# Scores, values and states of the sample rows on four column quarters, mixing biases from column sums, and scan rows scaled ahead of the norm

## The chip, the cores and the metric

One core of one Trainium2 chip runs the whole kernel as one program. The metric is the device time of one execution in microseconds; the kernel before was run three times. The engines are named as in the profile: PE is TensorE (matmuls; its weight loads are PEld), DVE is VectorE, ACT is ScalarE, POOL is GpSimd and SP is SyncE, which issues the DMAs here.

## The reference

One step of a hybrid decoder layer, for a prompt of 1024 positions and for 8 sample sequences of 4 positions each (32 rows), all in fp32, width 1024:

- `h = rmsnorm(x)`, and one input projection `h @ w_in` whose columns are split into the inputs of three branches.
- Branch A: `v = layernorm(gelu(v))`, then in chunks of 128 positions `mixed = w_s v + b_s` with a lower triangular `w_s` for each of 8 channel groups; out is `gelu(u) * mixed * silu(gate)`. As v is `xhat * g + b`, the part of `mixed` that comes from the layer norm's `b` is `b` times the row sums of `w_s`: together with `b_s` it is a bias that depends on channel and position only (the kernel's BM).
- Branch B: a causal convolution of width 4 with SiLU, then a chunked scan with 16 heads of 64 channels, 2 groups and a state of 128: inside a chunk `(C B^T * decay) (x dt)`, across chunks `C h`, and `h = decay h + B^T (x dt)`; then `y = (y + d_skip x) * silu(z)`, divided by its root mean square over each group's 512 channels and scaled by `ssm_norm_g`.
- Branch C: attention of 4 heads of 256 channels over 256 memory tokens, gated. The prompt uses keys and values projected from `mem_prompt`; each of the 8 sample sequences uses its own cached keys and values.
- `y = rmsnorm(x + concat(A, B, C) @ w_out)`. New states, convolution tails, memory keys and values, and the samples' v rows are returned too.

## The kernel before

The large projections are fp32 products made of three products each, of a high and a low part of both operands (`gemm3`, lines 339 to 341: high by high, high by low, low by high). The parts are made by `split` (L124 on ACT, L127 on DVE or POOL). After each step of the contraction `gemm3` calls `hook`: the counter grows by `pace["rate"]`, and for each whole number reached one step of the side work runs, that is, one generator goes on to its next `yield`. What a step issues lands in the engines' queues between main products. So the order on each engine is that of the text as this interleaving unrolls it, and every engine works its queue in order; a `yield` moves what follows it back by 1/rate hooks.

The main stages in order of time: load and norm of the rows with their transposes into pairs of high and low parts (`rn[t].s1a`, `s1b`, `s2`, to about 20 us), the projections of z and v, then the units that make a block product with 7 sub-products (`unit`), for the convolved columns from 225 to 360 us and for the queries and the two gates from 360 to 665 us. In that last stretch the side work is `side_chain` (L1768): `conv_samples`, `mem_prep`, `sample_scan`, `sample_scores`, `sample_values`, `gm_prep`, one after the other at rates of 1.25, and 0.32 in the stages with loads. Then come the units with the mixing products, the scan of the prompt between products of the gate (786 to 1003 us), the first output projection, the projection of the memory's keys and values with the loading and splitting of the scan's rows (L2104 to 2130), the second output projection with attention, and the last one with the final norm.

What the change touches:

- `samp_in` (L490) multiplies the 32 sample rows in four column tiles of 32 each, 256 columns at a time. It is not changed.
- `sample_scores` (L1569): 16 steps, each with a 512 KB load, 8 transposes of keys (L1602), two copies out of PSUM, and the products of two heads for the step before (L1587), 4 products in the two column tiles of these heads. An fp32 product stands in the trace as two records. `sample_values` (L1626) has 16 steps of 4 products (L1649) in the same way.
- `sample_scan` (L1360): for each of 8 sequences two products of 512 columns in column tiles 0 and 1 (L1469) collect `C h` in `accs`; then for each group `gate_norm` and after that the scaling.
- `gm_prep` (L1703): transposes of `w_s`, three operations of 32x1024 on DVE for the samples' v rows (L1738 to 1741), then BM from 16 products (L1746, L1747), of 128 rows of a broadcast `b` by `w_s` and of one row of ones by `b_s`.
- The scan (L1248) works on chunk i, while `sA(i + 1)` prepares the next. `gate_norm` (L1113) has a product on DVE, Square with a sum on ACT (L1120), and `rstd`. Rows of chunk i - 1 are transposed into a PSUM bank of the units (`y_T`), scaled on ACT out of it (`y_T2`, L1138, four parts) into the tile `sz`, and stored from there to `yb_d` (L1141). `sz` has one buffer and also takes the gate's load; `xsD` has three, and L1200 writes the one that is free next.

```python
r = y_T(p.xsD, 128, gp_, cp_ * 128, acc_bank())
...
s_.r = gate_norm(SC_.p, s_.xsD, sz, 128)
...
fs.append(y_T2(r, 128, gp_, cp_ * 128, sz))
```

- `loadB` and `splitB` (from L2076): loads of the scan's rows into three buffers; four tiles per group were kept in SBUF and stand in the same list.
- The tail: `rows_part` and `rows_fin` sum squares of the last block in parts that end at the column blocks named in `SQE`.

## Time and profile before

| | us |
|---|---|
| runs | 1336.42, 1339.17, 1339.26 (median 1339.17) |
| profiled execution | 1339.14 |
| its span in the profile | 1337.4 |
| PE busy | 1276.8 |
| DVE busy | 759.7 |
| ACT busy | 587.5 |
| POOL busy | 348.7 |

The span runs from the first to the last instruction of the profiled execution. Busy time is the sum over an engine's instructions, without overlaps; an engine that is busy for 95% of the span leaves 60 us in which it does nothing. A time line lists an engine's instructions with start, duration, engine, line, output and inputs by tile names, tile shape, and in brackets the idle time of the engine ahead of it with the instruction that ended it; with several instructions of one kind in a row, their count stands behind an x. The granted clock is given as a share of full speed, 2.4 GHz.

### The profile page before, as it was taken

How to read it: one execution, taken by the hardware profiler on the slowest of the kernel's cores; microseconds unless marked ns; L12 is line 12 of the kernel's file. 1: busy time of each engine (PE TensorE's matmuls, PEld its weight loads, DVE VectorE, ACT ScalarE, POOL GpSimd, SP SyncE). 2: the span in 40 equal slices, each digit the busy share in tenths (PEclk: the TensorE clock that was granted, in tenths of full speed). 3: DMA queues.
4: the chain of work that ended last, by engine and by line, in shares of the span. 5: the costliest groups of instructions: out<-in, count | busy, mean ns of one | idle time of the engine just before them, and what ended most of it. 6: DMA issues, size and time to landing. Idle time of an engine off the chain costs nothing.

```text
span 1337.4 us, 22025 instructions
## 1 busy us (share of the span) xinstructions
PE 1276.8 (95%) x8211; PEld 1075.5 (80%) x8211; DVE 759.7 (57%) x1258; ACT 587.5 (44%) x1227; POOL 348.7 (26%) x384
## 2 busy tenths in 40 slices
...
GB/s 242 75 84 98 139 93 46 88 106 102 125 176 159 190 109 268 119 233 155 109 194 165 201 200 164 76 126 127 175 89 150 267 230 220 170 191 245 179 139 98
DMA packets 210622, 204.68 MB, mean 153 GB/s; under 512 B 28124, under 2 KB 176688, under 8 KB 209492
## 3 DMA queue, kind: packets, MB, share of 16 engines
...
q8 instruction: 65, 1.06, 0.3%
...
q0 software_dynamic: 512, 0.13, 0.1%
...
## 4 chain that ended last, share of the span: by engine, by line
PE 73%; DVE 9%; DMA 8%; ACT 4%; issue 3%; POOL 2%; SPq 1%; POOLq 0%; ACTq 0%; DVEq 0%
PE ps_mm L339 19%; PE ps_mm L341 18%; PE ps_mm L340 18%; DVE ul L457 1%; PE ps_acc L1649 1%; PE ps_acc L1587 1%; DMA yb<-yb_d 1%; PE ps_sd L1849 1%; PE ps_sd L1602 1%; DMA sz<-z_d 1%; DMA y_d<-gt 1%; DMA cr<-c_d 1%; PE ps_sd L317 1%; PE ps_sd L1293 1%; PE ps_acc L490 1%
## 5 line engine op out<-in xcount | busy, mean ns | idle before, releaser
L449 ACT ACTIVATE uh<-wst 128x512 fp32r<-128x512 f32 x80 | 50.1, 628 | 96.1 <-PE ps_mm L340 77.6
L457 DVE TENSOR_TENSOR ul<-wr,uh 128x512 fp32r<-128x512 f32 x84 | 68.4, 814 | 39.8 <-ACT uh L449 39.8
L2370 POOL TENSOR_TENSOR xres<-xres,gfin 128x1536 f32<-128x1536 f32 (+3 forms) x6 | 14.4, 2396 | 274.9 <-DVE ys L2418 233.8
L127 DVE TENSOR_TENSOR wl<-wr,wh 128x512 fp32r<-128x512 f32 (+3 forms) x53 | 51.2, 987 | 60.7 <-ACT wh L124 60.1
L449 ACT ACTIVATE uh<-wr 128x512 fp32r<-128x512 f32 x84 | 52.4, 625 | 59.7 <-PE ps_mm L340 55.3
L457 DVE TENSOR_TENSOR ul<-wst,uh 128x512 fp32r<-128x512 f32 x80 | 61.4, 767 | 23.3 <-ACT uh L449 23.0
L339 PE MATMUL ps_mm<-bH,wh 128*128 128x384 f32 (+1 forms) x192 | 63.6, 331 | 3.8 <-ACT bH L124 3.8
L340 PE MATMUL ps_mm<-bL,wh 128*128 128x384 f32 (+1 forms) x192 | 62.2, 324 | 0.3 <-DVE bL L127 0.3
L341 PE MATMUL ps_mm<-bH,wl 128*128 128x384 f32 (+1 forms) x192 | 62.1, 323 | 0.0
L435 POOL TENSOR_TENSOR wst<-wr 128x512 f32<-128x512 f32 x20 | 26.9, 1343 | 124.9 <-DMA wr<-in_w_in_dram 38.7
L124 ACT ACTIVATE wh<-wr 128x512 fp32r<-128x512 f32 (+3 forms) x60 | 47.3, 815 | 25.0 <-PE ps_mm L340 13.6
L339 PE MATMUL ps_mm<-xT1H,uh 128*128 128x512 f32 x128 | 54.6, 426 | 2.0 <-ACT uh L449 2.0
L339 PE MATMUL ps_mm<-xB22H,uh 128*128 128x512 f32 x128 | 53.9, 421 | 1.5 <-ACT sz_s L1120 1.0
L1016 DVE SCALAR_TENSOR_TENSOR ps_sd<-raw,vecs,ps_sd 128x512 f32<-128x512 f32 x72 | 54.2, 752 | 1.7
L339 PE MATMUL ps_mm<-xB21H,uh 128*128 128x512 f32 x128 | 53.6, 419 | 1.2 <-ACT uh L449 1.2
L339 PE MATMUL ps_mm<-xB11H,uh 128*128 128x512 f32 x128 | 52.3, 409 | 0.0
L340 PE MATMUL ps_mm<-xT1L,uh 128*128 128x512 f32 x128 | 52.0, 406 | 0.0
L341 PE MATMUL ps_mm<-xT1H,ul 128*128 128x512 f32 x128 | 51.9, 405 | 0.1
L340 PE MATMUL ps_mm<-xB21L,uh 128*128 128x512 f32 x128 | 51.0, 398 | 0.0
L341 PE MATMUL ps_mm<-xB21H,ul 128*128 128x512 f32 x128 | 50.9, 397 | 0.0
L340 PE MATMUL ps_mm<-xB22L,uh 128*128 128x512 f32 x128 | 50.8, 397 | 0.0
L341 PE MATMUL ps_mm<-xB22H,ul 128*128 128x512 f32 x128 | 50.6, 395 | 0.0
...
## 6 DMA issues: line engine op xcount, KB each, us to landing
...
```

Of the source, the lines that this page charges most:

```text
L124: ACT.activation(out=H, in_=raw, func=AF.Copy)
L127: leng.tensor_tensor(out=L, in0=raw, in1=rb(H), op=ALU.subtract)
L317: PE.transpose(out=ps[:, i, :T], in_=self.xn[:T, k * 128:(k + 1) * 128], identity=ident[:T, :T])
L339: PE.matmul(out=ps, lhsT=lH, rhs=rH, start=(first and k == k0), stop=False)
L340: PE.matmul(out=ps, lhsT=lH, rhs=rL, start=False, stop=False)
L341: PE.matmul(out=ps, lhsT=lL, rhs=rH, start=False, stop=(last and k == k0 + kn - 1))
L435: POOL.tensor_tensor(out=t1, in0=A_(u, 2, 1), in1=A_(u, 2, 2), op=ALU.add)
L449: ACT.activation(out=h, in_=src, func=AF.Copy)
L457: eng.tensor_tensor(out=l, in0=src, in1=rb(h), op=ALU.subtract)
L490: PE.matmul(out=ps[32 * j:32 * j + 32, 0:256], lhsT=xs[:, 4 * r + j, :], rhs=R[r][:, j, :], start=(r == 0), stop=(r == 1), tile_position=( ...
L1016: DVE.scalar_tensor_tensor(out=ps, in0=raw[:, 512 * h + j:512 * h + j + 512], scalar=cw(ct, j), in1=ps, op0=ALU.mult, op1=ALU.add)
L2370: eng.tensor_tensor(out=t[:, 0:nf, c0:c0 + w], in0=t[:, 0:nf, c0:c0 + w], in1=gc.unsqueeze(1).to_broadcast([128, nf, w]), op=ALU.mult)
```

## The change

Eleven transposes of the identity are issued in three places of the start. Steps are added: four ahead of the samples' SiLU, one net in the loop that makes the samples' xdt, three ahead of their `gate_norm` (one behind it goes), three in `gm_prep`. The rate of the side work goes from 1.25 to 1.32, and in the values' stage from 0.32 to 0.16, where a step now does twice the work. Scores and values take all four heads of a sequence at once, in four column tiles; the state products take four tiles of 256 columns. BM comes from column sums of the transposed `w_s` (a product with a column of ones), copied into row 0 of r2, over `b_s` in row 1, and one product of two rows by g2, whose row 0 is `b` and row 1 is ones. In the scan `y_T2` is issued before the norm of the next chunk, and writes into the `xsD` it came from; the order of the three products of `C h` is turned; `lt_make` goes from DVE to ACT. Half of the low parts in `a_split` go from POOL to DVE. Kept rows are split directly, so that the three buffers serve loads alone from the first step on. The tail's parts end at column blocks 3, 6, 7.

```diff
@@ -643,6 +643,12 @@
+    def turn(n):
+
+        ps = acc_bank()
+        for _ in range(n):
+            PE.transpose(out=ps[:, 0:128], in_=ident, identity=ident)
+
@@ -700,8 +706,11 @@
     x_s1a(1)
+    turn(7)
     rn[0].s2(0)
+    turn(2)
     rn[0].s2(1)
+    turn(2)
     w_split(2)
@@ -1043,6 +1052,8 @@
             yield
+        for _ in range(4):
+            yield
         ACT.activation(out=cvs, in_=cvs, func=AF.Silu)
@@ -1065,7 +1076,7 @@
                 PE.transpose(out=ps[:27, i * 128:(i + 1) * 128], in_=csT[:, 4 * j + i, :], identity=ident)
-            csn = pool.tile([128, 512], F32, tag="csn", name="csn", bufs=2)[:27]
+            csn = pool.tile([128, 512], F32, tag="csn", name="csn", bufs=3)[:27]
             ACT.activation(out=csn, in_=ps[:27, :], func=AF.Copy)
@@ -1169,7 +1180,7 @@
             t = Lts[i] = SC_.p.tile([128, 128], F32R, tag="Lt", name="Lt", bufs=2)
-            DVE.tensor_scalar(out=t, in0=SB_.Lraw, scalar1=SB_.qmask[:, i % 4:i % 4 + 1], scalar2=None, op0=ALU.mult)
+            ACT.activation(out=t, in_=SB_.Lraw, func=AF.Copy, scale=SB_.qmask[:, i % 4:i % 4 + 1])
             l_rows(i + 4)
@@ -1274,7 +1285,9 @@
                 po = sd()
-                mm3(po, s_.CH, s_.CL, *hHL)
+                PE.matmul(out=po, lhsT=s_.CH, rhs=hHL[0], start=True, stop=False)
+                PE.matmul(out=po, lhsT=s_.CL, rhs=hHL[0], start=False, stop=False)
+                PE.matmul(out=po, lhsT=s_.CH, rhs=hHL[1], start=False, stop=True)
             else:
@@ -1309,20 +1322,19 @@
                 sE(i + 1, 1)
+            fs = []
             if i > 0:
...
                 r = y_T(p.xsD, 128, gp_, cp_ * 128, acc_bank())
+                fs.append(y_T2(r, 128, gp_, cp_ * 128, p.xsD))
             DVE.tensor_tensor(out=s_.xsD, in0=s_.xsD, in1=pd, op=ALU.add)
...
                 DVE.tensor_tensor(out=hHL[1], in0=hT, in1=rb(hHL[0]), op=ALU.subtract)
-            fs = []
             if c == 7:
                 fs.append(state_out(g))
-            if i > 0:
-                fs.append(y_T2(r, 128, gp_, cp_ * 128, sz))
             yield
@@ -1412,8 +1424,8 @@
             DVE.tensor_tensor(out=h3(xsD[:, cs]), in0=h3(ps[:32]), in1=hb(dsk_b[:32, 8 * j:8 * j + 8], 32, 8), op=ALU.mult)
-        for _ in range(2):
-            yield
+            yield
+        yield
         DVE.tensor_tensor(out=h3(xde), in0=h3(xdt), in1=hb(te_s, 32, NH), op=ALU.mult)
@@ -1465,9 +1477,10 @@
                     ACT.activation(out=hbt[:, k, :], in_=hbt[:, k, :], func=AF.Copy, scale=decT[:, k, b:b + 1])
-                for g in range(2):
-                    PE.matmul(out=accs[32 * g:32 * g + 32, :], lhsT=Cm[:, g, b * 32:(b + 1) * 32],
-                              rhs=hTb[g], start=(b == 0), stop=(b == 7), tile_position=(0, 32 * g))
+                for q in range(4):
+                    PE.matmul(out=accs[32 * q:32 * q + 32, 0:256], lhsT=Cm[:, q // 2, b * 32:(b + 1) * 32],
+                              rhs=hTb[q // 2][:, (q % 2) * 256:(q % 2 + 1) * 256], start=(b == 0), stop=(b == 7),
+                              tile_position=(0, 32 * q))
             ps = sd()
@@ -1496,7 +1509,7 @@
         f()
-        set_pace(1.25)
+        set_pace(1.32)
         sz_s = sp2.tile([128, 8, 128], F32, tag="hb", name="sz_s", bufs=4).rearrange("p k n -> p (k n)")[:32]
@@ -1507,12 +1520,15 @@
                           start=True, stop=True)
-            DVE.tensor_copy(out=t1[:, cs], in_=accs[32 * g:32 * g + 32, :])
+            for e in range(2):
+                q = 2 * g + e
+                DVE.tensor_copy(out=t1[:, q * 256:(q + 1) * 256], in_=accs[32 * q:32 * q + 32, 0:256])
             DVE.tensor_tensor(out=h3(t1[:, cs]), in0=h3(t1[:, cs]), in1=hb(ea_s[:, 8 * g:8 * g + 8], 32, 8), op=ALU.mult)
...
             DVE.tensor_tensor(out=xsD[:, cs], in0=xsD[:, cs], in1=t1[:, cs], op=ALU.add)
+            for _ in range(3):
+                yield
             rs.append(gate_norm(sp2, xsD[:, cs], sz_s[:, cs], 32))
-            yield
             yield
@@ -1580,20 +1596,19 @@
-        def scores(b, a):
-            kTb = kTs.pop((b, a))
+        def scores(b):
+            kT = [kTs.pop((b, a)) for a in range(2)]
             for dt in range(2):
-                for h in (2 * a, 2 * a + 1):
+                for h in range(4):
                     PE.matmul(out=psS[h * 32:(h + 1) * 32, :], lhsT=qm[:, 2 * h + dt, b * 32:(b + 1) * 32],
-                              rhs=kTb[:, 2 * (h - 2 * a) + dt, :], start=(b == 0 and dt == 0), stop=(b == 7 and dt == 1),
+                              rhs=kT[h // 2][:, 2 * (h % 2) + dt, :], start=(b == 0 and dt == 0), stop=(b == 7 and dt == 1),
                               tile_position=(0, h * 32))
-        prev = None
         for b in range(8):
...
                 kb = kvq.pop(0)
-                kTb = sap.tile([128, 4, 256], F32, tag="kTb", name="kTb", bufs=2)
+                kTb = sap.tile([128, 4, 256], F32, tag="kTb", name="kTb", bufs=3)
                 for j in range(2):
@@ -1606,12 +1621,11 @@
                 kTs[b, a] = kTb
-                if prev is not None:
-                    scores(*prev)
-                prev = (b, a)
+                if b and not a:
+                    scores(b - 1)
                 yield
-        scores(*prev)
-        set_pace(1.25)
+        scores(7)
+        set_pace(1.32)
         yield
@@ -1638,20 +1652,20 @@
             yield
-        set_pace(0.32)
+        set_pace(0.16)
         psO = acc_bank()[:, 0:256]
         for b in range(8):
-            for a in range(2):
-                kv_load()
-                vb = kvq.pop(0)
-                for m in range(2):
-                    for h in (2 * a, 2 * a + 1):
-                        PE.matmul(out=psO[h * 32:(h + 1) * 32, :], lhsT=pm[:, m, h, b * 32:(b + 1) * 32],
-                                  rhs=vb[:, m, (h - 2 * a) * 256:(h - 2 * a + 1) * 256], start=(b == 0 and m == 0),
-                                  stop=(b == 7 and m == 1), tile_position=(0, h * 32))
-                yield
+            vb = [kvq.pop(0) for _ in range(2)]
+            for m in range(2):
+                for h in range(4):
+                    PE.matmul(out=psO[h * 32:(h + 1) * 32, :], lhsT=pm[:, m, h, b * 32:(b + 1) * 32],
+                              rhs=vb[h // 2][:, m, (h % 2) * 256:(h % 2 + 1) * 256], start=(b == 0 and m == 0),
+                              stop=(b == 7 and m == 1), tile_position=(0, h * 32))
+            kv_load()
+            kv_load()
+            yield
         DVE.tensor_copy(out=Psm, in_=psO)
-        set_pace(1.25)
+        set_pace(1.32)
         yield
@@ -1710,22 +1724,26 @@
             wsp = pp.tile([128, 8, 128], F32, name="wsp")
-            bsr = pp.tile([1, D], F32, name="bsr")
-            one_r = pp.tile([1, 128], F32, name="one_r")
+            g2 = pp.tile([2, D], F32, name="g2")
+            r2 = pp.tile([2, D], F32, name="r2")
+            one_c = pp.tile([128, 1], F32, name="one_c")
             rep = pp.tile([4, 8, 4], F32, name="rep")
-            gnb_b = pp.tile([128, D], F32, name="gnb_b")
+            gnb_b = pp.tile([32, D], F32, name="gnb_b")
             gng_b = pp.tile([32, D], F32, name="gng_b")
...
             SP.dma_start(out=wsp, in_=gm_w_spatial[0].rearrange("h t s -> t h s"))
-            SP.dma_start(out=gnb_b, in_=gm_norm_b.to_broadcast([128, D]))
+            POOL.memset(g2, 1.0)
+            SP.dma_start(out=g2[0:1], in_=gm_norm_b)
+            SP.dma_start(out=gnb_b, in_=gm_norm_b.to_broadcast([32, D]))
             SP.dma_start(out=gng_b, in_=gm_norm_g.to_broadcast([32, D]))
-            SP.dma_start(out=bsr, in_=gm_b_spatial[0].rearrange("h t -> (h t)").unsqueeze(0))
+            SP.dma_start(out=r2[1:2], in_=gm_b_spatial[0].rearrange("h t -> (h t)").unsqueeze(0))
             SP.dma_start(out=G.vsn, in_=v_d[NP:NT, :])
-            POOL.memset(one_r, 1.0)
+            POOL.memset(one_c, 1.0)
             POOL.memset(rep, 1.0)
...
             yield from conv_out(pp)
+            yield
             yield
@@ -1738,13 +1756,19 @@
             DVE.tensor_tensor(out=vs, in0=G.vsn, in1=gng_b, op=ALU.mult)
-            DVE.tensor_tensor(out=vs, in0=vs, in1=gnb_b[:NS], op=ALU.add)
+            DVE.tensor_tensor(out=vs, in0=vs, in1=gnb_b, op=ALU.add)
+            for j in range(2):
+                ps = sd()
+                PE.matmul(out=ps[0:1, :], lhsT=one_c, rhs=WT[:, 4 * j:4 * j + 4, :].rearrange("p h t -> p (h t)"),
+                          start=True, stop=True)
+                DVE.tensor_copy(out=r2[0:1, j * 512:(j + 1) * 512], in_=ps[0:1, :])
+            yield
+            yield
             for j in range(2):
...
                 for i in range(4):
-                    h = 4 * j + i
-                    PE.matmul(out=ps[:, i, :], lhsT=gnb_b[:, h * 128:(h + 1) * 128], rhs=WT[:, h, :], start=True, stop=False)
-                    PE.matmul(out=ps[:, i, :], lhsT=one_r, rhs=bsr[:, h * 128:(h + 1) * 128], start=False, stop=True)
+                    hs = slice((4 * j + i) * 128, (4 * j + i + 1) * 128)
+                    PE.matmul(out=ps[:, i, :], lhsT=g2[:, hs], rhs=r2[:, hs], start=True, stop=True)
                 DVE.tensor_copy(out=BM[:, 4 * j:4 * j + 4, :], in_=ps)
@@ -1787,7 +1811,7 @@
         pace["acc"] = 0.0
-        set_pace(1.25)
+        set_pace(1.32)
@@ -1974,7 +1998,7 @@
                 ACT.activation(out=H, in_=src, func=AF.Copy)
-                U.late.append((L, src, H, POOL if e else DVE))
+                U.late.append((L, src, H, DVE))
         return f
@@ -2070,20 +2094,22 @@
     ybp = yb_ctx.enter_context(tc.tile_pool(name="ybp", bufs=1, side="right"))
-    ytodo = ([(1, c) for c in range(KEEP, 8)] + [(g, c) for c in range(4) for g in range(2)] +
-             [(0, c) for c in range(4, NTILE)] + [(1, 8)])
+    ytodo = ([(g, c) for c in range(KEEP) for g in range(2)] +
+             [(0, c) for c in range(KEEP, NTILE)] + [(1, 8)])
...
             ytodo.pop(0)
-            if g and KEEP <= c < 8:
-                ybs.append((g, c, SC_.y[c].rearrange("p (k t) -> p k t", k=4)))
-                return
             t = ybp.tile([128, 4, 128], F32, tag="yb", name="yb", bufs=3)
...
             ybs.append((g, c, t))
+
+    def splitK(n):
+        c = KEEP + n
+        ts_ = slice(c * 128, c * 128 + 128)
+        split(SC_.y[c].rearrange("p (k t) -> p k t", k=4), bH[:, 4:8, ts_], bL[:, 4:8, ts_], ACT, DVE)
@@ -2118,11 +2144,11 @@
             if n < 4:
-                loadB()
-                splitB(0)
-            elif n < 15:
+                splitK(n)
+            if n < 15:
                 splitB(2)
-                loadB()
+                if n not in (3, 7, 11):
+                    loadB()
             else:
@@ -2398,7 +2424,7 @@
     side2 = Side()
-    SQE = [3, 5, 7]
+    SQE = [3, 6, 7]
     wo_get()
```

## Rows read from the trace of the kernel before

**Rows 1.** From the page: busy time of the engines, with share of the span and instructions; and the shares of the chain that ended last, by engine.

```profile
PE 1276.8 (95%) x8211; PEld 1075.5 (80%) x8211; DVE 759.7 (57%) x1258; ACT 587.5 (44%) x1227; POOL 348.7 (26%) x384
...
PE 73%; DVE 9%; DMA 8%; ACT 4%; issue 3%; POOL 2%; SPq 1%; POOLq 0%; ACTq 0%; DVEq 0%
```

**Rows 2.** The waits of PE: line, the instruction waited for, us in total, times, longest.

```profile
PE ps_acc L479 <- ACT sz L1138: 7.7, 2, 5.1
PE ps_sd L1287 <- DVE BL L127: 6.4, 6, 1.8
```

**Rows 3.** Time line of PE, in the stage of the samples' scores: a visit with transposes only, one of the products of four column tiles, one with transposes and scores, each with the main product that follows.

```profile
506.54 1.03 PE L1602 MATMUL ps_sd<-ident,kv 128*128 128x128 f32 x8
507.33 0.49 PE L339 MATMUL ps_mm<-xB21H,uh 128*128 128x512 f32 x1
...
540.71 1.07 PE L490 MATMUL ps_sd<-wr,xsr 128*32 128x256 f32 x16
...
541.71 0.50 PE L339 MATMUL ps_mm<-xT2H,uh 128*128 128x512 f32 x1
...
543.89 1.03 PE L1602 MATMUL ps_sd<-ident,kv 128*128 128x128 f32 x8
...
544.85 1.06 PE L1587 MATMUL ps_acc<-kTb,qm 128*32 128x256 f32 x8
...
545.84 0.50 PE L339 MATMUL ps_mm<-xT2H,uh 128*128 128x512 f32 x1
```

**Rows 4.** Time line of PE: state products of the sample scan, and a group of the values' stage with the main product behind it.

```profile
476.66 1.05 PE L1469 MATMUL ps_acc<-hTb,Cm 128*32 128x512 f32 x4
...
477.64 1.11 PE L1474 MATMUL ps_sd<-Bm,X 96*128 96x128 f32 x8
...
585.85 1.06 PE L1649 MATMUL ps_acc<-kv,pm 128*32 128x256 f32 x8
...
586.84 0.50 PE L339 MATMUL ps_mm<-xT3H,uh 128*128 128x512 f32 x1
```

**Rows 5.** Busy time by window: the window, its length, busy us and instructions of PE, PEld, DVE, ACT and POOL, then the granted clock, the DMA share and GB/s.

```profile
16.00:17.00 1.00, 1.00 (x6) 1.00 (x6) 1.00 (x3) 1.00 (x2) 0.00 (x0) 1.00 1.02 307
66.00:99.00 33.00, 33.00 (x281) 32.91 (x281) 6.03 (x9) 9.43 (x20) 0.00 (x0) 1.00 0.25 73
594.00:627.00 33.00, 33.00 (x182) 20.15 (x180) 11.00 (x17) 5.93 (x10) 5.15 (x4) 1.00 0.66 210
656.00:657.00 1.00, 1.00 (x5) 0.56 (x3) 1.00 (x1) 0.00 (x0) 0.10 (x1) 0.50 0.49 173
866.00:867.00 1.00, 1.00 (x6) 0.75 (x3) 1.00 (x3) 0.88 (x2) 0.27 (x1) 0.50 0.87 233
1056.00:1089.00 33.00, 28.93 (x213) 27.91 (x212) 20.65 (x34) 19.71 (x40) 0.00 (x0) 1.00 1.06 289
```

**Rows 6.** Time line of PE and DVE in `gm_prep`: the first of the 16 products of BM, one of the 32x1024 operations on DVE, and the main product that follows the last of the 16.

```profile
651.17 0.38 PE L1746 MATMUL ps_sd<-WT,gnb_b 128*128 128x128 f32 x2
...
657.21 1.21 DVE L1741 TENSOR_TENSOR vs<-vs,gnb_b 32x1024 f32<-32x1024 f32 x1
...
659.11 0.80 PE L339 MATMUL ps_mm<-xB22H,uh 128*128 128x512 f32 x1
```

**Rows 7.** Time line of PE and DVE at the start: the first transposes of normed rows, and the low part of the second tile.

```profile
12.52 1.11 PE L317 MATMUL ps_sd<-ident,xn 128*128 128x128 f32 x4 [0.91 <-DVE xn L309]
...
16.66 0.68 DVE L127 TENSOR_TENSOR xB21L<-ps_sd,xB21H 128x512 fp32r<-128x512 f32 x1
```

**Rows 8.** Time line of ACT and PE in the side chain: the samples' SiLU, and three main products with an idle PE ahead of them.

```profile
371.90 0.52 ACT L1046 ACTIVATE cvs<-cvs 128x384 f32<-128x384 f32 x1 [8.56 <-POOL cvs L1044]
373.00 0.50 PE L339 MATMUL ps_mm<-xT1H,uh 128*128 128x512 f32 x1 [1.99 <-ACT uh L449]
...
487.70 0.47 PE L339 MATMUL ps_mm<-xB22H,uh 128*128 128x512 f32 x1 [0.99 <-ACT sz_s L1120]
...
493.26 0.47 PE L339 MATMUL ps_mm<-xT4H,uh 128*128 128x512 f32 x1 [2.59 <-DVE go L508]
```

**Rows 9.** Time line in the scan: Square, the scaling of rows and the PE instruction that needs their bank, a Square of the next iteration, and a store of rows with the DVE write of xsD behind it (SPq is SP's queue of issues).

```profile
861.72 0.63 ACT L1120 ACTIVATE sz<-xsD 128x512 f32<-128x512 f32 x1 [4.27 <-DVE xsD L1118]
...
862.48 1.14 ACT L1138 ACTIVATE sz<-ps_acc,vecs 128x128 f32<-128x128 f32 x4
...
863.67 0.69 PE L479 MATMUL ps_acc<-ident,se 128*128 128x128 f32 x2 [5.06 <-ACT sz L1138]
...
877.76 0.62 ACT L1120 ACTIVATE sz<-xsD 128x512 f32<-128x512 f32 x1
...
891.38 0.37 SPq L1141 DMA_DIRECT2D yb_d<-sz  x1
...
893.84 0.68 DVE L1200 TENSOR_TENSOR xsD<-ps_sd,dsk_b 128x512 f32<-128x512 f32 x1
```

**Rows 10.** The chain that ended last, in order of time: start, us, what.

```profile
921.43 6.18 DMA yb_d<-sz
```

**Rows 11.** Time line of PE at the start of the second output projection.

```profile
1079.87 0.44 PE L339 MATMUL ps_mm<-bH,wh 128*128 128x384 f32 x1 [1.22 <-ACT bH L124]
...
1087.43 0.40 PE L339 MATMUL ps_mm<-bH,wh 128*128 128x288 f32 x1 [2.56 <-ACT bH L124]
```

**Rows 12.** Time line of DVE in the tail.

```profile
1329.45 0.16 DVE L2380 TENSOR_REDUCE rs<-sq 128x3 f32<-128x9 f32 x1 [1.53 <-ACT junk L2364]
```

## The prediction

> **What bounds the kernel now.** I read the page's busy times first, then its chain, then the waits of TensorE, then the time lines of the stages that the change touches. PE is busy 95% of the span and holds 73% of the chain that ended last [rows 1]. So a change is worth what it does to PE: products taken from its queue, idle gaps in front of it, and the stretches in which its clock is halved. The other engines count only where PE waits for them, or where they would come to make it wait. The two waits of PE that the change is near stand in [rows 2]: 7.7 us in two gaps on ScalarE's scaling of scan rows, and 6.4 us in six gaps at the end of the chain that runs through the norm. The profiled run took 1339.14 us, 1.74 us of it outside the span; the median of the runs is 1339.17, so sums made against the profile hold for the median as they stand, and the fastest of the three lies 2.7 us lower.
>
> **Scores and values on four column tiles.** In the K stage a small visit is priced by the distance to the next main product. A visit of transposes alone takes 507.33 − 506.54 = 0.79 us; one of transposes and scores takes 545.84 − 543.89 = 1.95; so a scores group (8 records on two tiles) costs 1.16 [rows 3]. What 16 records on four tiles cost is shown by L490, which has the same 128x256 operands: 541.71 − 540.71 = 1.00 [rows 3]. Twice the work on twice the tiles costs the same. The change makes 8 groups of 16 records out of 16 of 8, with the loads, transposes and steps of the K stage unaltered: −8 x 1.16 = **−9.3 us**. In the values stage a group of 8 records on two tiles takes 586.84 − 585.85 = 0.99 [rows 4], and 8 of 16 go: **−7.9**. Its rate is halved with the number of steps, so loads come at the same mean rate, but in pairs. Over that stage DMA is at 0.66 of its engines [rows 5], and by the code two tiles are always loaded ahead of the pair in use; I cost the pairing at nothing, and if that cover is gone the gain of the stage is (rival D). The higher rate elsewhere (1.32 for 1.25) is there to fit some more steps into the same products; I count 188 steps, done two hooks ahead of the end of the stage.
>
> The state products of the sample scan (L1469) keep their 8 visits, of 0.98 us each [rows 4], but go from 4 records of 512 columns on two tiles to 8 of 256 on four. A 256-column product takes 33 / 281 = 0.117 us [rows 5], and 512 columns less on each tile are 0.23: 8 x 0.23 = **−1.8**. The bounds are 0 (the visit's cost is fixed) and 8 x 0.49 = −3.9, if the visit halves, as 8 records are half of what L490 does in 1.00. The table in "Theoretical Speedup" of the Trainium skill's page "TensorEngine Tiling (Array Packing)" lets small tiles of up to 32 columns run up to four at once; by it the sum would be 2.1 us lower, at that outer bound.
>
> **Mixing biases (gm_prep).** The stretch from the first of the 16 products to the next main product takes 659.11 − 651.17 = 7.94 us [rows 6], and part of it runs at half clock (granted 0.50 in 656:657, that is 1.2 GHz [rows 5]). The new form has 8 products of two rows, 16 records: as two visits of the price of the eight transposes, 2 x 0.79 = 1.6, and two column sums of 512 columns, four records, some 1.3 with the 0.98 of L1469 as the nearest row. So 7.94 − 2.9 = −5.0, and −1.8 of half clock should go with it. Against that stands a new wait: the second products read r2, which DVE copies out of the column sums, and that copy is issued behind three 32x1024 operations, each 1.21 us long [rows 6]; two added steps cover about 1 us of the 3.6. I charge +2.5 for it. Together **−4** (bounds −7 and −1: cover complete, or the wait and the low clock both stay). g2's and r2's loads and memset go out early in the part, on queues that nobody near waits for.
>
> **Waiting steps of the sample chain.** Before, ScalarE's Silu at 371.90 waits 8.56 us for the convolution on POOL, the main split of uh is queued behind it on ScalarE, and PE stands 1.99 us [rows 8]. Four more steps are some 3 hooks, at three main products to a hook and 0.4 to 0.5 us each about 4 us of cover: **−1.8** (0 to −2). gate_norm's Square and its rstd likewise hold ScalarE and DVE, and PE stands 0.99 and 2.59 [rows 8]; three steps ahead of it let its inputs arrive, yet the DVE chain behind it (product, reduction, rstd) is no shorter: **−2** (0 to −3.6). The third csn buffer, and the step in the loop at L1408, I cost at nothing: no gap of PE ends there.
>
> **Start.** Eleven transposes of the identity go in where PE waits 0.91 us for DVE's xn [rows 7]. In 16:17 only 6 main products start in a us [rows 5], against 33 / 281 us a product of half that width later. If the extra work fills the idle gap, the products behind it come at full pace sooner; but tile 1's low part is ready only at 16.66 + 0.68 = 17.34 [rows 7], so little is to be had: **−0.8** (−1.2 to +0.5, the upper end if the 11 transposes at 0.79 / 8 = 0.10 us each lie in front of s2). Part 4, "PE-mode transpose", of the Trainium skill's page "TensorE: Matmul & The Clock Gate" says that the high clock doesn't engage for transposes; no run here shows it yet, and by it this term gives nothing (rival G).
>
> **Scan.** This is the widest term. In an iteration ScalarE's Square waits 4.27 us for DVE (861.72), the four scalings of the rows of the iteration before come after it (862.48, 1.14 us), and PE, which needs the same PSUM bank, stands 5.06 us until 863.67 [rows 9]. Moved ahead of Square, the scalings would run in the 4.27 us in which ScalarE has nothing to do, and that gap falls away, as would the other of [rows 2], with their half clock (0.50 at 866:867 [rows 5]): −7.3 and −1.5. The price is where ScalarE wasn't idle: Square at 877.76 has no idle time in front of it [rows 9], and so starts up to 1.14 later; behind it are rstd, the scaled matrix, BH, BL and the wait of L1287 that PE has six times already [rows 2]. Some four such iterations: +4. Next, scaled rows now go into xsD's buffer, and its store must have read them before DVE's L1200 writes that buffer again. Before, the store went out at 891.38 and DVE's write came at 893.84, 2.46 us later [rows 9]; +1 for the cases that are a little late. The order of the three products of one sum changes nothing but that hL is wanted one product later; lt_make moves to ScalarE, 128x128, cheaper than one of the four parts in 1.14 us; a_split's low half moves from POOL to DVE: all ~0, as no gap of PE ends on them. Together **−4** (−10 to +8).
>
> **yb loads.** At the start of the second output projection PE stands 1.22 and 2.56 us for the split of late yb tiles [rows 11]. The loads now begin at the first step, since the kept tiles no longer hold a place among the three, and by the last step 13 of 14 are in, not 12: **−2.5** (0 to −4; the DMA engines are full there, share 1.06 at 289 GB/s [rows 5], and speak for the upper end).
>
> **Tail.** The last part is 128 columns wide, the one before 384: DVE's 1.53 us wait for ScalarE's squares [rows 12] gets shorter, POOL's wider product lies ahead of rstd. **0** (±0.5).
>
> **Sum.** −9.3 − 7.9 − 1.8 − 4 − 1.8 − 2 − 0.8 − 4 − 2.5 = −34.1; 1339.1 − 34.1 = **1305 us** (forecast A, chance 0.45).
>
> **Rivals.**
> B, every stall goes whole, its half clock with it: −19.0 (K, V, state products), −7, −2, −3.6, −1.2, −10, −4 give −46.8, 1292 us. For it: the gaps have single named releasers. Against: 6.4 us of L1287 show that another chain is close behind. 0.16.
> C, only the products go: −19.0, and each removed gap comes back at the next dependency, since the chains behind are no shorter: 1320 us. For it the same L1287; against it that most gaps are order on one engine, not length of a chain. 0.20.
> D, the values stage runs at the pace of its loads in pairs (0.66 share, 210 GB/s [rows 5]) and gives 7.9 back: 1313 us. 0.05.
> E, slower: the store that reads xsD holds up DVE's L1200, with all of the scan behind it. One store took 6.18 us on the chain of waits [rows 10], against a slack of 2.46: 3.7 us late, and if all 12 stores that are not kept did so, 12 x 3.7 = 44, 1349 us, more with low clock. It decides from 34.1 / 12 = 2.8 us per store. Three buffers, and most stores not on the chain, speak against. 0.04.
> F, the change doesn't do what it says: the four tiles don't run side by side in these operands, a group of 16 costs two of 8, and 19 us stay: 1324 us. L490 speaks against. 0.03.
> G, transposes of the identity don't help the clock: the start term becomes 0 to +0.5, 1306 us. 0.05.
> The last 0.02 is for no difference.
>
> **How the numbers follow.** Predicted 1305. All lower ends at once are −49.4, all upper ones about 1330; the range takes in B's side to 1290 and C with 3 us more, 1323: outside are E, F, the last 0.02, a little of C and B, some 0.14. A measurement of this kernel tells about 0.2%, 2.7 us, from no change. A, B, C, D, F and G are faster by more: 0.94; the same 0.02; slower 0.04.
>
> **What would show it.** K: 8 groups of 16 records at about 1.0 us, the other visits at 0.79; V: 8 groups. If these take about 2 us, F. The 7.94 of gm_prep becomes 4 to 5; a PE gap on r2 there is the charged wait. The two L479 gaps gone from PE's waits; a longer L1287 is the charge on Square; a DVE wait of L1200 on a DMA is E. The gaps at 373, 488, 493, 1080 and 1087 smaller or moved. The forecast is wrong above all if the scan term falls outside its bounds.

## The result, and the profile after

The changed kernel takes 1305.56 us (median of 4 runs, 1303.47 to 1307.84) against 1339.22 of the kernel before, taken beside it (median of 4, 1336.42 to 1343.37). The ratio is 0.9747, with a 95% interval of 0.9715 to 0.9779: 33.7 us less. The forecast was 1305. The profiled run took 1306.92, with a span of 1305.2, 32.2 less than the span before.

Busy time by engine and the shares of the chain that ended last, from the page of the changed kernel (before: [rows 1]):

```profile
PE 1252.2 (96%) x8242; PEld 1067.7 (82%) x8242; DVE 755.0 (58%) x1250; ACT 589.6 (45%) x1243; POOL 340.8 (26%) x381
...
PE 73%; DVE 9%; DMA 6%; ACT 5%; issue 3%; POOL 2%; SPq 1%; POOLq 0%; ACTq 0%; DVEq 0%
```

PE is busy 24.6 us less, and the span lost 32.2: about three quarters of the gain is work or half clock (stretches with a granted clock of 0.50, 1.2 GHz) taken from PE, the rest idle time. The sum agrees with the forecast; whether its terms do must be read elsewhere. Both kernels issue the main products in the same order, so the n-th run of main products with a given left operand can be found in both time lines, and the difference of its start times is the **shift** at that place. What a stretch gives is how the shift grows in it:

| stretch (ends at, before / after) | forecast | shift at its end | the stretch gave |
|---|---|---|---|
| start and first projections (219.59 / 219.06) | -0.8 | -0.5 | -0.5 |
| SiLU, state products, gate_norm of the samples (503.69 / 497.97) | -5.6 | -5.7 | -5.2 |
| scores (578.05 / 563.35) | -9.3 | -14.7 | -9.0 |
| values (642.22 / 619.03) | -7.9 | -23.2 | -8.5 |
| gm_prep (667.09 / 646.58) | -4 | -20.5 | **+2.7** |
| units with mixing, then scan (1003.59 / 973.81) | -4 | -29.8 | **-9.3** |
| keys and values, yb, second projection (1224.14 / 1193.35) | -2.5 | -30.8 | -1.0 |
| last projection and tail (spans 1337.4 / 1305.2) | 0 | -32.2 | -1.4 |

Two terms were wrong, by 6.7 and 5.3 us in opposite directions. The waits of PE show both (line, waited for, us in total, times, longest; before: [rows 2]):

```profile
PE ps_sd L1300 <- DVE BL L127: 10.1, 10, 2.1
...
PE ps_sd L1771 <- DVE r L1764: 3.8, 1, 3.8
...
PE ps_sd L1290 <- DVE hL L1335: 1.3, 3, 0.6
...
PE ps_acc L479 <- ACT xsD L1149: 0.8, 2, 0.5
```

The 7.7 us on the scaling have become 0.8. L1300 is the L1287 of before, and its 6.4 us have become 10.1: most of that is the charge for a later Square (experiment 3), which the forecast put at +4. L1771 are the new mixing products, which wait for r2.

Small visits in the time line of PE after (before: [rows 3, 4]; a count in the last row of a window takes in only the records that start before its end): the state products and what follows; a scores group and a values group, each with the main product behind it.

```profile
447.10 0.64 PE L1481 MATMUL ps_acc<-hTb,Cm 128*32 128x256 f32 x8
...
447.67 0.55 PE L1487 MATMUL ps_sd<-Bm,X 96*128 96x128 f32 x3
...
507.69 1.07 PE L1603 MATMUL ps_acc<-kTb,qm 128*32 128x256 f32 x16
...
508.69 0.50 PE L339 MATMUL ps_mm<-xT3H,uh 128*128 128x512 f32 x1
...
574.83 1.07 PE L1661 MATMUL ps_acc<-kv,pm 128*32 128x256 f32 x16
...
575.83 0.50 PE L339 MATMUL ps_mm<-xB22H,uh 128*128 128x512 f32 x1
```

A group of 16 records takes 1.00, as L490 had shown, and there are 8 of each kind. A group of state products takes 447.67 - 447.10 = 0.57 in place of 0.98: 8 x 0.41 = 3.3 us, near the outer bound of 3.9.

Time line of DVE and PE in gm_prep after (before: [rows 6]), then the window 636:637 (length, busy us of PE, PEld, DVE, ACT, POOL, granted clock, DMA share, GB/s):

```profile
628.75 1.88 PE L1762 MATMUL ps_sd<-WT,one_c 128*1 128x512 f32 x4
...
631.21 2.17 DVE L1758 TENSOR_TENSOR vs<-vsn,gng_b 32x1024 f32<-32x1024 f32 x1
...
633.41 1.21 DVE L1759 TENSOR_TENSOR vs<-vs,gnb_b 32x1024 f32<-32x1024 f32 x1
634.56 1.27 DVE L1764 COPY r<-ps_sd 1x512 f32<-1x512 f32 x2
635.28 1.00 PE L1771 MATMUL ps_sd<-r,g 2*128 2x128 f32 x3 [3.76 <-DVE r L1764]
...
637.28 0.80 PE L339 MATMUL ps_mm<-xB22H,uh 128*128 128x512 f32 x1
```

```profile
636.00:637.00 1.00, 1.00 (x7) 1.00 (x5) 0.42 (x1) 0.00 (x0) 0.00 (x0) 0.50 0.72 266
```

The three 32x1024 operations on DVE run from 629.50 to 634.62, 5.1 us where I took 3 x 1.21. The copy into r2 starts when the last of them ends, PE stands 3.76 us, and after the gap the granted clock is 0.50: the first visit of 8 records, which are 4 products, takes 637.28 - 635.28 = 2.00 us, not the 0.79 that I gave it.

### The profile page after: what moved, and what is told of

Its sections match the earlier page's. It is cut to its first block, busy times and chain, and to the rows that moved or that the text cites. A ratio compares the mean times of both kernels' runs of the same rounds, so it can differ in the third digit from the quotient of the medians.

```text
span 1305.2 us, 22101 instructions
## 1 busy us (share of the span) xinstructions
PE 1252.2 (96%) x8242; PEld 1067.7 (82%) x8242; DVE 755.0 (58%) x1250; ACT 589.6 (45%) x1243; POOL 340.8 (26%) x381
## 3 DMA queue, kind: packets, MB, share of 16 engines
q8 instruction: 65, 1.06, 0.3%
## 4 chain that ended last, share of the span: by engine, by line
PE 73%; DVE 9%; DMA 6%; ACT 5%; issue 3%; POOL 2%; SPq 1%; POOLq 0%; ACTq 0%; DVEq 0%
PE ps_mm L339 20%; PE ps_mm L341 19%; PE ps_mm L340 19%; PE ps_sd L1873 1%; POOL MT L1250 1%; PE ps_sd L1617 1%; DVE ul L457 1%; PE ps_sd L1306 1%; PE ps_sd L317 1%; DMA qr<-q_d 1%; ACT sz L1131 1%; PE ps_sd L490 1%; PE ps_acc L1661 1%; PE ps_acc L1603 1%; PE ps_acc L490 1%
```

## The experiments

Each is timed beside the kernel before, whose median lay between 1339 and 1343 us from experiment to experiment, so ratios are compared: 0.001 is 1.34 us, and the changed kernel stands at 0.9747. Shifts are those of main products against the changed kernel, unless another is named.

**1. Column sums first (e1_sums_first).**

```diff
             yield
+            (both column sums and their copies into r2)
             DVE.tensor_scalar(out=G.vsn, ...)
             DVE.tensor_tensor(out=vs, in0=G.vsn, in1=gng_b, op=ALU.mult)
             DVE.tensor_tensor(out=vs, in0=vs, in1=gnb_b, op=ALU.add)
-            (both column sums and their copies into r2)
```

> The changed kernel with the two column sums and their copies into r2 issued ahead of the three 32x1024 operations on DVE, nothing else. In the changed kernel PE stands 3.76 us for r2, the granted clock is 0.50 from about 636 to 643.6 us, and the mixing-bias part lies 2.7 us worse than before on PE. Theory (the wait is the queue on DVE, and the low clock follows the idle gap): the 3.76 goes but for some tenths, the two visits of 8 products fall from 2.0 to about 1.0 us each, no low clock: 7 to 9 us less than the changed kernel, about 1298. Rival (the products of two rows bring the clock down by themselves): only the gap goes, the low clock stays, 3 to 4 us less, about 1302. Rival (the gap comes back as a wait for a PSUM bank whose copy is now behind the three operations): no gain, 1305.

1299.07 us, ratio 0.9673 (0.9639 to 0.9707); the shift over gm_prep is -7.6. Time line, and the window 628:636 in the columns of above:

```profile
631.79 0.68 DVE L1760 COPY r<-ps_sd 1x512 f32<-1x512 f32 x1 [0.18 <-PE ps_sd L1758]
...
632.58 1.15 PE L1771 MATMUL ps_sd<-r,g 2*128 2x128 f32 x8
...
633.66 0.50 PE L339 MATMUL ps_mm<-xB22H,uh 128*128 128x512 f32 x1
```

```profile
628.00:636.00 8.00, 8.00 (x39) 4.80 (x38) 7.04 (x9) 0.63 (x1) 3.16 (x2) 1.00 0.55 176
```

The wait is gone, the clock stays at 1.00, and a visit of 8 records (4 products; there are two visits) takes 633.66 - 632.58 = 1.08. So the products of two rows don't bring the clock down by themselves: in the changed kernel it took the gap ahead of them. With the wait covered the part gives 2.7 - 7.6 = -4.9.

**2. Old order of the three products (e2_hl_order).**

```diff
-                PE.matmul(out=po, lhsT=s_.CH, rhs=hHL[0], start=True, stop=False)
-                PE.matmul(out=po, lhsT=s_.CL, rhs=hHL[0], start=False, stop=False)
-                PE.matmul(out=po, lhsT=s_.CH, rhs=hHL[1], start=False, stop=True)
+                mm3(po, s_.CH, s_.CL, *hHL)
```

> The changed kernel with the old order of the three products of C h in the scan (low part of h second, not last). Theory A: the waits for hL, 5.2 us before and 1.3 after, fell because hL is wanted one product later; they come back, 3 to 4 us more than the changed kernel, about 1309. Theory B: they fell because DVE has less ahead of hL (lt_make on ACT, scaling elsewhere): within 1 us of the changed kernel, and the wait for hL stays under 2 us.

1305.81 us, 0.9741 (0.9704 to 0.9778); the wait for hL is 2.0 us. The order is worth nothing that can be seen: theory B, as the forecast had it.

**3. Scaling behind Square again (e3_scale_late).**

```diff
-                fs.append(y_T2(r, 128, gp_, cp_ * 128, p.xsD))
             DVE.tensor_tensor(out=s_.xsD, in0=s_.xsD, in1=pd, op=ALU.add)
...
+            if i > 0:
+                fs.append(y_T2(r, 128, gp_, cp_ * 128, p.xsD))
             yield
```

> The changed kernel with the scaling of scan rows issued again after the Square of the next chunk (still into xsD). Theory (the order on ACT is what the scan gained from): the wait of L479 on the scaling goes from 0.8 back to about 7.7 us with some low clock, the wait on BL from 10.1 to about 6.4: 4 to 6 us more, about 1311. Rival (the gain of the scan is from the other edits in it, the order of the products and lt_make): L479 stays under 3 us, and the time within 2 us of the changed kernel.

1312.28 us, 0.9783 (0.9752 to 0.9815): +4.8 by the ratio, and the shift grows from 1.2 at 776 to 5.7 at 994. Waits of PE:

```profile
PE ps_sd L1300 <- DVE BL L127: 7.5, 7, 2.1
PE ps_acc L479 <- ACT xsD L1149: 5.4, 2, 3.1
```

The early scaling is worth some 4.5 us, the -4 of the forecast, and of the 10.1 us at L1300 it had added 2.6. But L479 comes back to 5.4, not 7.7: part of the old gap was something else's.

**4. Tiles in pairs (e4_pairs).**

```diff
-            for dt in range(2):
-                for h in range(4):
+            for dt, h in ((0, 0), (0, 1), (1, 0), (1, 1), (0, 2), (0, 3), (1, 2), (1, 3)):
```

and the same for the values.

> The changed kernel with the 8 products of a scores group, and of a values group, issued as 4 on the column tiles 0 and 1 and then 4 on the tiles 2 and 3, in place of all four tiles in turn: same products, same visits. Theory (four tiles run side by side when neighbours in the queue are on different tiles): a visit has two stretches of two tiles, each like the groups of the kernel before without the change of shape, so 1.0 becomes 1.6 to 2.0 us and 16 visits give 9 to 16 us more, about 1315 to 1321. Rival (a visit costs about 1 us, whatever is in it, so only the number of visits counts): within 2 us of the changed kernel.

1306.4 us, 0.9741 (0.9711 to 0.9771), and no shift in either stage. A scores group takes 506.69 - 505.67 = 1.02:

```profile
505.67 1.08 PE L1603 MATMUL ps_acc<-kTb,qm 128*32 128x256 f32 x16
506.69 0.50 PE L339 MATMUL ps_mm<-xT3H,uh 128*128 128x512 f32 x1
```

What I expected of the theory was wrong: neighbours in the queue need not be on different tiles. That leaves a fixed price per visit, or four tiles that each work through their own products whatever the order; experiment 7 tells these apart.

**5. Two buffers for cbm (e5_cbm_two).**

```diff
-        s_.cbm = SC_.p.tile([128, 128], F32, tag="cbm", name="cbm", bufs=1)
+        s_.cbm = SC_.p.tile([128, 128], F32, tag="cbm", name="cbm", bufs=2)
```

The chain behind L1300, in the time line of the changed kernel:

```profile
851.88 1.28 POOL L1250 TENSOR_TENSOR MT<-MT,cbm 128x512 f32<-128x512 f32 x1
...
853.20 0.29 DVE L1208 TENSOR_TENSOR cbm<-ps_sd,triu 128x128 f32<-128x128 f32 x1 [2.16 <-POOL MT L1250]
...
853.83 0.29 DVE L127 TENSOR_TENSOR BL<-ps_sd,BH 128x128 fp32r<-128x128 f32 x1 [0.34 <-ACT BH L124]
...
854.17 0.50 PE L1300 MATMUL ps_sd<-xdH,BH 128*128 128x512 f32 x1 [0.97 <-DVE BL L127]
```

> The changed kernel with two buffers for cbm in the scan, not one. In the changed kernel PE waits 10.1 us in ten gaps for BL; ahead of BL on DVE stands the write of the next cbm, which waits some 2.2 us for POOL's product that reads the old one, and POOL gets to that only behind rstd of the norm. Theory (the chain Square, rstd, POOL's product, cbm, BH, BL is what the earlier scaling pushes later): with a second buffer cbm is written at once, the ten gaps fall under 3 us, 6 to 9 us less than the changed kernel, about 1298. Rival (the gaps come back at the next thing that POOL or ACT owes, the scaled matrix itself): 0 to 3 us less.

1293.91 us, 0.9639 (0.9601 to 0.9677): 14 us less than the changed kernel, more than expected. The scan's part of the shift goes from -0.8 at 776 to -15.4 at 974, and the waits show why:

```profile
PE ps_sd L1300 <- DVE BL L127: 1.1, 1, 1.1
```

DVE had stood still for a buffer, not for data, and far longer than PE shows. Its wait in the changed kernel, 28.5 us in the kernel before, and gone here:

```profile
DVE cbm L1208 <- POOL MT L1250: 29.0, 13, 2.9
```

From 646.58 to 973.81 in the changed kernel, the part of the table with the scan, PE now idles 9.7 us less and is busy 4.8 us less with the same products; I estimate 1.7 of the 4.8 from half clock (10.2 us in the changed kernel, 6.8 here, at half the pace); the rest isn't taken apart.

**6. lt_make on DVE again (e6_lt_dve).**

```diff
-            ACT.activation(out=t, in_=SB_.Lraw, func=AF.Copy, scale=SB_.qmask[:, i % 4:i % 4 + 1])
+            DVE.tensor_scalar(out=t, in0=SB_.Lraw, scalar1=SB_.qmask[:, i % 4:i % 4 + 1], scalar2=None, op0=ALU.mult)
```

> The changed kernel with lt_make on DVE again. Theory A: the wait for hL fell from 5.2 to 1.3 us since DVE has one operation less ahead of it; it comes back by 2 to 4 us, and so does the time. Theory B: it fell because the gate's load came earlier in the two iterations in which DVE stood 3 us for it; then hL stays under 2.5 us, and the time is within 2 us of the changed kernel.

1310.54 us, 0.976 (0.9721 to 0.9798); the wait for hL rises from 1.3 to 2.1, and the shift grows by 2.4 between 776 and 889. By the ratio that is 1.7 us, which its interval can't tell from nothing, and by the wait it is theory B. Half clock lasts 6.8 us behind 835 here and 3.4 in the changed kernel, which is most of the 2.4, so no price of lt_make is shown. The wait for hL had been longer before:

```profile
PE ps_sd L1218 <- DVE hL L1320: 5.2, 3, 2.8
```

No single edit brings that back: it is 2.0 with the old order, 2.1 here, 2.7 in experiment 3 and 2.8 in experiment 9, so what took it to 1.3 stays open.

**7. Two tiles only (e7_two_tiles).** In the values' stage, heads 2 and 3 write the other half of the bank from the tiles of heads 0 and 1 (the start and stop flags and the copy out of the bank follow suit).

```diff
-                    PE.matmul(out=psO[h * 32:(h + 1) * 32, :], ...
+                    PE.matmul(out=psO[h % 2 * 32:(h % 2 + 1) * 32, h // 2 * 256:(h // 2 + 1) * 256], ...
-                              ... tile_position=(0, h * 32))
+                              ... tile_position=(0, h % 2 * 32))
```

> The changed kernel, in the values' stage alone: the same 8 visits with the same 8 products, but heads 2 and 3 on column tiles 0 and 1 too, into the other half of the bank. Only two tiles are used. Theory A (each tile works through its own products, side by side with the others, at about 0.23 us a record of 256 columns, in any order): 8 records a tile, a visit takes 1.0 + 4 x 0.23 = 1.9 us, eight visits 7.5 us more than the changed kernel, about 1313. Theory B (a visit costs about 1 us whatever is in it): within 1.5 us of the changed kernel, and visits of 1.0.

1311.85 us, 0.9768 (0.9725 to 0.9811). The profile is sharper than the ratio: the shift grows by 6.3 us over the eight visits, by 0.78 to 0.85 at each but the first, and a group takes 585.57 - 583.71 = 1.86:

```profile
583.71 1.92 PE L1661 MATMUL ps_acc<-kv,pm 128*32 128x256 f32 x16
...
585.57 0.50 PE L339 MATMUL ps_mm<-xT4H,uh 128*128 128x512 f32 x1
```

Theory A. The time of a visit is that of its fullest tile: 4 records a tile take 1.0 and 8 take 1.86; the state products, with 2 a tile, take 0.57. Carried on to no records, these three leave some 0.14 us a visit that doesn't depend on their number, an estimate.

**8. Both repairs (e8_both):** the edits of 1 and 5 together.

> The changed kernel with both repairs: the column sums ahead of the three operations of 32x1024, and two buffers for cbm. The one alone gave a ratio to the kernel before of 0.9673, the other 0.9639, against 0.9747 of the changed kernel. They lie 130 us apart in the time line. If they add: 0.9747 - 0.0074 - 0.0108 = 0.9565, about 1281 us against 1339. Rival (the second takes part of what the first frees, since both end at DVE's queue): 0.960 or more.

1287.76 us, ratio 0.9596 (0.9576 to 0.9616): the fastest kernel of this study, 4.0% under the kernel before and 18 to 20 us under the changed one. Gm_prep's shift of -7.6 and the scan's, from -8.2 to -21.4, are both there (7.6 and 14.6 alone). The sum expected, 0.9565, lies just outside the interval. The scan gives 1.4 less than alone, with 10.2 us of half clock where experiment 5 has 6.8; 1.3 come back between the scan and the last projection and 1.1 in it, for which no cause is shown.

**9. Four small places undone (e9_small_undone).**

```diff
-    turn(7)
...
-                U.late.append((L, src, H, DVE))
+                U.late.append((L, src, H, POOL if e else DVE))
...
-                splitK(n)
...
-    SQE = [3, 6, 7]
+    SQE = [3, 5, 7]
```

> The changed kernel without the transposes of the identity at the start, with the old order of the yb loads, the old ends of the tail's parts, and the low half of a_split on POOL again: four places that lie far apart, each read from the time line by the shift of the main products against the changed kernel. Forecast terms: start 0.8, yb 2.5, tail 0, a_split 0. By the profile of the changed kernel: start 0.5, the stretch of the memory's keys and second output projection 0.75, the last projection and tail 1.4, of which 0.9 is a wait for a weight's low part that no edit names. Theory: 0.5 to 1 at the start, 0.7 to 2.5 at the yb tiles, under 0.5 in the tail; 1307 in all. Rival (the 1.4 at the end is the tail's new ends): over 1 us in the last 30 us.

1315.22 us, 0.9794 (0.9757 to 0.983): 6 us more, where 1.5 was expected. Start: the shift at 219 is +0.3, and it lies between -0.2 and +1.5 in the nine profiles that keep the transposes, so nothing is shown. Yb: +2.2 (0.7 to 2.5 expected). Tail: about +0.5. The rest is a_split, which the forecast had at nothing: the shift goes from -0.6 at 776 to +5.8 at 858. PE idles only 2.1 us more in that stretch; the rest is busy time, as half clock lasts 13.7 us in it and 3.4 in the changed kernel.

**10. a_split alone, in the kernel before (e10_asplit_alone).**

```diff
-                U.late.append((L, src, H, POOL if e else DVE))
+                U.late.append((L, src, H, DVE))
```

> The kernel before with the second half of a_split's low parts on DVE, not POOL, nothing else. Without that edit and three others the changed kernel lost 6 to 7 us between 775 and 860 us, where a_split runs; the forecast had it at nothing. Theory A (the two halves side by side hold each other up, DVE's half takes 3.2 to 3.4 us beside POOL's and 1.2 alone, and the norm is queued behind both): alone it gives 4 to 7 us in 836 to 866 us, part of the 5.06 wait of L479, a ratio of about 0.996. Theory B (it counts only since rows are scaled early, as the POOL chain then sets the end): under 1.5 us alone.

1336.96 us, ratio to the kernel before 0.9964 (0.9949 to 0.998): 4.8 us less (3.4 by the spans), from that one line. That is theory A by the time, but L479 goes only from 7.7 to 6.8; experiment 11 shows where the rest lies. The shift against the kernel before falls by 3.6 between 836 and 866. The time line of the kernel before:

```profile
840.42 1.23 DVE L457 TENSOR_TENSOR xB11L<-aB,xB11H 128x1024 fp32r<-128x1024 f32 x1
...
856.48 2.81 POOL L457 TENSOR_TENSOR xB22L<-aB,xB22H 128x1024 fp32r<-128x1024 f32 x1
...
856.98 3.38 DVE L457 TENSOR_TENSOR xB22L<-aB,xB22H 128x1024 fp32r<-128x1024 f32 x1
```

and of the changed kernel:

```profile
832.94 2.35 DVE L457 TENSOR_TENSOR xB22L<-aB,xB22H 128x1024 fp32r<-128x1024 f32 x2
```

A half takes 1.23 on DVE alone. Issued beside POOL's half it takes 3.38, ending 1.07 behind POOL's; DVE does both halves in 2.35, and is free a microsecond sooner than with POOL's help. The Trainium skill's page "SBUF — State Buffer", section "SBUF: two separate sides", says that DVE operations with two SBUF inputs and GpSimd operations that read SBUF hold one pair of ports exclusively, so that the second waits for the end of the first; the row agrees, as 859.29 (POOL's end) plus one half alone is 860.5, and DVE's ended at 860.36.

**11. Two cbm buffers alone, in the kernel before (e11_cbm_alone):** the edit of 5.

> The kernel before with two buffers for cbm, nothing else. It tells whether the chain through POOL was there before. Theory (the same wait: 6.4 us in six gaps at L1287, behind POOL's read of the old cbm): the gaps go and the time falls by 5 to 7 us, ratio about 0.996. Rival (before, the scaling behind Square sets the end in most chunks, and the gaps move to L479 or hL): under 3 us, and L479 or L1218 grows.

1327.89 us, 0.9899 (0.9884 to 0.9913): 13.5 less, twice what was expected. Waits of PE:

```profile
PE ps_acc L479 <- ACT sz L1138: 8.6, 2, 5.7
...
PE ps_sd L1218 <- DVE hL L1320: 4.4, 2, 2.6
...
PE ps_sd L1287 <- DVE BL L127: 1.1, 1, 1.1
```

The chain was there before and cost more than its 6.4 us of gaps; L479 takes back 0.9. The rest is half clock. Windows over the stretch with the scan, from the same main product to the same, in the kernel before, in experiment 10 and here:

```profile
667.09:1003.59 336.50, 309.35 (x1913) 238.06 (x1911) 223.81 (x356) 200.66 (x419) 127.11 (x143) 0.96 0.49 151
```

```profile
668.39:998.91 330.52, 304.26 (x1913) 234.51 (x1911) 221.77 (x360) 200.26 (x419) 116.66 (x139) 0.98 0.50 153
```

```profile
670.23:991.82 321.59, 301.61 (x1912) 235.10 (x1910) 227.03 (x357) 199.78 (x420) 127.30 (x143) 0.98 0.52 158
```

PE idles 27.2, 26.3 and 20.0 us, and the same products keep it busy 309.4, 304.3 and 301.6, as half clock lasts 27.3 us before and 13.7 in both others. So of the 6.0 us that experiment 10 gives in this stretch of its profile nearly all is half clock, and of this one's 14.9 about half. How much half clock a kernel gets differs between profiles, and each of these is one. This one buffer is worth more than all that the change did in the scan (9.3).

**12. Without the waiting steps (e12_no_steps).**

```diff
-        for _ in range(4):
-            yield
         ACT.activation(out=cvs, in_=cvs, func=AF.Silu)
...
-            for _ in range(3):
-                yield
             rs.append(gate_norm(sp2, xsD[:, cs], sz_s[:, cs], 32))
+            yield
             yield
```

> The changed kernel without the four steps ahead of the samples' SiLU and with gate_norm of the samples placed as in the kernel before (no steps ahead, two behind); the rate stays. Theory: PE stands again about 2 us behind the SiLU, and 1 us more near gate_norm; the shift of the main products against the changed kernel is +2 at the SiLU and, where the changed kernel still stands 2.1 us behind gate_norm, between +0.5 and +2: 3 to 4 us in all, ratio about 0.977. Rival (steps only move a stall to the next place in the side chain): the shift is back under 1 us by 500 us, and the time within 1.5 us of the changed kernel.

1303.95 us, 0.9717 (0.9679 to 0.9755): not slower than with the steps. The gap at the SiLU is back, in the time line of this kernel:

```profile
373.74 0.79 PE L339 MATMUL ps_mm<-xT1H,uh 128*128 128x512 f32 x1 [1.97 <-ACT uh L449]
```

The shift grows by 1.9 there, as the theory has it, and is +10 at 409. Then it falls by 6.2 until 422, since with the steps in, a later part of the side chain meets other work, and PE stands behind it in the changed kernel, at half clock for most of 12 us after. The gap, and the window 410:422 of the changed kernel (the granted clock is the third number from the end; in this kernel it is 1.00):

```profile
409.47 0.47 PE L339 MATMUL ps_mm<-xB22H,uh 128*128 128x512 f32 x1 [1.90 <-DVE go L508]
```

```profile
410.00:422.00 12.00, 12.00 (x46) 9.47 (x44) 4.12 (x8) 4.27 (x9) 4.84 (x4) 0.58 0.71 198
```

The profiles of experiments 2, 4, 5 and 8, which keep the steps and have the gap, lose 3 to 5 us less than that of the changed kernel just there: half clock behind the same gap lasts from nothing (experiment 5) to 13.7 us (experiment 7).

At 498 the shift is +4.5, where it was +1.5 at 219. PE idles 10.1 us in that stretch, 6.4 in the changed kernel and 11.0 before; 1.2 of the 10.1 is a wait for keys whose visit comes one step earlier. So the steps do save PE some 2.5 us of waiting. That is made up for in gm_prep: between 498 and 647 the changed kernel needs 148.6 us and this one 142.5 (0.8 of the difference is that visit). The side chain is further on here, its three DVE operations take 0.79, 1.21 and 1.21, a visit of L490 lies between the column sums and the products, and r2 is there in time:

```profile
627.35 1.27 DVE L1761 COPY r<-ps_sd 1x512 f32<-1x512 f32 x2
...
628.72 1.15 PE L1768 MATMUL ps_sd<-r,g 2*128 2x128 f32 x8
...
629.80 0.50 PE L339 MATMUL ps_mm<-xT2H,uh 128*128 128x512 f32 x1
```

PE doesn't stand for r2, and the granted clock is 1.00 throughout. The shift is -1.6 at 647 and -1.1 at 974. So the steps covered the waits that they were put in for, as the theory says, and by this profile they also moved gm_prep to a place where its own wait lay open. That is the rival's idea, but neither its sign (under 1 us by 500) nor the theory's total came true. (In between, the shifts also hold work that the side chain does earlier or later.)

## Why the prediction was right, and where its steps were not

- **Scores and values**: right, -9.0 and -8.5 for -9.3 and -7.9. Two rows of before gave both, and experiment 7 shows the reason. D and F are out: the pairs of loads show in the first visit of the values alone, which takes 1.95 us with 0.33 of waiting for a load in it, and four tiles do run side by side.
- **State products**: the mechanism was right and the size was not: -3.3 measured, -1.8 taken. I took 0.117 us for 256 columns from main products, which are of another kind; an fp32 record of 256 columns takes 0.21 on its tile (experiment 7: 0.86 for four more). The outer bound, which the Trainium skill's page "TensorEngine Tiling (Array Packing)" gave in "Theoretical Speedup" with up to four tiles at once, was nearer.
- **gm_prep**: the failed step is "+2.5 for it", with "−1.8 of half clock should go with it". The queue ahead of r2 was named rightly but priced at three times the 1.21 of the one row shown; it took 5.1, as the first operation took 1.67 and the second 2.17. The gap of 3.76 brought half clock back, and the new products were paid at that clock: two visits of 2.00, where 1.6 was taken for both. A wait that PE really makes can't be charged beside a clock that is taken as whole. The work was priced low as well: the column sums take 1.8 us for 1.3, and the two visits 2 x 1.08 even at full clock. So experiment 1, with the wait covered, gives -4.9, not the -7 of the forecast's bound, and experiment 12, without the steps of the chain ahead, has no wait for r2 either.
- **Waiting steps**: the waits were right, the gain of -1.8 and -2 is not seen in the time. The stretch gave -5.2 for -5.6, but 3.3 of that are state products. PE idles 11.0 us there before and 6.4 after, of which experiment 12 lays some 2.5 to the steps; against that the profile after has 10.2 us of half clock there, the one before 3.4. The cover was also taken twice too long: main products of 512 columns start 0.23 us apart at full clock, and 0.4 to 0.5 is the length of their records, so four steps are about 2.1 us, not 4, just enough for the gap of 1.99. And by experiment 12 the steps cost in gm_prep what they saved ahead of it. The rate of 1.32 and the third csn buffer are undone in no experiment; their part isn't shown.
- **Start**: -0.5 for -0.8, but neither is shown, as experiment 9 says. The products of 16:17 and of 66:99 both have 256 columns; the first are not twice as wide, as the forecast has it, but run at half the pace. Windows 13:17 of the kernel before, then of the changed one:

```profile
13.00:17.00 4.00, 4.00 (x20) 4.00 (x20) 3.28 (x4) 1.79 (x3) 1.66 (x3) 1.00 0.75 199
```

```profile
13.00:17.00 4.00, 3.40 (x28) 2.98 (x26) 3.29 (x4) 2.48 (x5) 2.04 (x4) 1.00 0.62 165
```

  28 records take 3.40 us where 20 took 4.00, so PE is at full pace behind the transposes, and then idles 0.6 for normed rows and a low part (the granted clock reads 1.00 in both windows). The Trainium skill's page "TensorE: Matmul & The Clock Gate", Part 4, has it that the high clock doesn't engage for transposes (rival G); that is not borne out here, though the time shows next to nothing of it: four transposes of rows take 1.06 us and the next four 0.65, with nothing but transposes of the identity (L650) between.

```profile
7.71 1.06 PE L317 MATMUL ps_sd<-ident,xn 128*128 128x128 f32 x4
...
8.99 0.65 PE L317 MATMUL ps_sd<-ident,xn 128*128 128x128 f32 x4
```

  The pace doesn't always hold: of the ten profiles with the transposes, six have 3.4 us at a granted clock of 0.50 somewhere between 13 and 19 us (experiments 1, 4, 5, 6, 8 and 12), and of the four without them, none.
- **Scan**: the total of -4 failed by its zeros, "all ~0, as no gap of PE ends on them". a_split was worth 4.8 alone, in the kernel before, and 4 to 6 in the changed one (the lower by the ratio of experiment 9 less its 2.7 for yb and tail, the upper by its time line); the early scaling 4.5, as priced; lt_make 2 at most. Undone one at a time they sum to 8 to 13, and together they gave 9.3, so whether they overlap is not shown. Half clock itself was priced at -1.5 from one window, but before it lasts 27.3 us in this stretch and after 10.2, so some 4 of the 9.3 us are PE's busy time (309.4 to 305.4), and 5.4 its idle time. Part of the 5.06 us that I laid to the order on ScalarE was DVE's 3.38 behind POOL: the wait names the last releaser, not what had made it late. The charge of +4 on Square was 10.1 - 6.4 = 3.7, of which experiment 3 ties 2.6 to the early scaling; experiments 5 and 11 show that the wait behind it was one for cbm's buffer, which the forecast didn't ask about.
- **Rival E** is seen once in twelve stores. DVE's late rows reach PE by way of ScalarE, which waits 3.82 us for DVE's hT at 901.01, and PE then stands 1.08 at 902.89 for a matrix that is made behind it; the rows are from the changed kernel:

```profile
894.07 0.50 SPq L1152 DMA_DIRECT2D yb_d<-xsD  x1
...
898.49 0.69 DVE L1211 TENSOR_TENSOR xsD<-ps_sd,dsk_b 128x512 f32<-128x512 f32 x1 [3.43 <-DMA yb_d<-xsD]
```

- **yb**: -2.2 by experiment 9, -2.5 forecast. In the table the stretch gives -1.0, since a wait for qL is new behind it (before: [rows 11]):

```profile
1054.60 0.40 PE L339 MATMUL ps_mm<-bH,wh 128*128 128x288 f32 x1 [1.49 <-ACT bH L124]
...
1062.26 0.38 PE L2196 MATMUL ps_sd<-kH,qL 128*128 128x256 f32 x1 [1.05 <-DVE qL L127]
```

- **Tail**: 0 was right for the new ends. DVE's wait for the squares is 1.26 (1.53 before, [rows 12]). The 1.4 in the table is mostly a weight's low part that no longer comes 0.9 late at 1234, which no edit names.

So the number was better than its working: gm_prep and the steps gave some 8 us less than forecast, the scan and the state products 7 more. That the sum came within 1 us of the measured time is luck; what holds of it is scores and values, 17.5 us where 17.2 were forecast, and the early scaling.
